# Gate vectors written as rows, an entry with two tiles' first products, and conditioning vectors spread over the heads

## Chip, cores and metric

One program on one core of a Trainium2 chip. The metric is device time in microseconds (us) of one execution; three runs of the kernel before gave a median of 1038.4 us (1037.4 to 1039.1).

## The reference

One layer on a sequence of 512 tokens of width 1024, in float32: a half-weight SwiGLU feed-forward (FFN1), a token mixing with four mLSTM heads and four HGRN2 heads, and a second half-weight feed-forward (FFN2). Each sub-layer normalises its input, scales and shifts it with vectors computed from a conditioning vector `c`, and adds its normalised output through a gate that comes from `c` too:

```python
sc = jax.nn.silu(c)
mod = (sc @ ada_w[l] + ada_b[l])[:, None, :]
(sh1, sc1, g1, sh2, sc2, g2, sh3, sc3, g3) = jnp.split(mod, N_MOD, axis=-1)

y = rmsnorm(h, ffn1_pre_g[l]) * (1.0 + sc1) + sh1
y = swiglu(y, ffn1_w_gate[l], ffn1_w_up[l], ffn1_w_down[l])
h = h + FFN_RESIDUAL_WEIGHT * g1 * rmsnorm(y, ffn1_post_g[l])
# the same with sh2, sc2, g2 around token_mix (no half weight), and with sh3, sc3, g3 around the second swiglu
```

## The kernel before

Every weight matrix is multiplied in a split form: a tile is loaded raw (512 KB for 128 partitions x 1024), ScalarE (ACT) writes its rounded part `h_...`, VectorE (DVE) the remainder `l_...`, and TensorE (PE) makes three matmuls for each product, high by high (L111), low by high (L112), high by low (L113). Raw tiles, conditioning blocks included, go round four buffers, split pairs round four more; loads are issued by SyncE (SP) in program order, each when its buffer is free. Each engine runs its queue in order; a scheduler put the instructions into that order by their place in the program and by what they depend on, and an instruction that waits holds everything behind it on its engine.

**FFN tiles (`seven`, L262 to L401).** The first three of 22 feature tiles of a feed-forward are plain products. From tile 3 on, a tile is made with seven half-size products (`p1` to `p7`), all of 128x256 outputs, 12 matmuls each, in two accumulators `pA` and `pB`. The names end in the tile: `pAa3` is `pA` of FFN1's tile 3, `pAb3` of FFN2's. A tile's raw halves are `Ra` and `Rb`. `prep1` splits `Ra` (`h1`, `l1`) and rounds half of `Rb` (`h4`); `prep2` forms differences of `Ra` and `Rb` in place (L312 to L315), `prep3` and `prep4` split these (`h3`, `l3` and `h2`, `l2`), `prep5` makes `l4` with an accumulating load. `open` takes the accumulators. `p1` and `p2` need only `h1`, `l1` and the activations; `p6`, `p5`, `p7` need sums of activations too (`Shi`, `Slo`, `S[2]`) and `h2`, `h3`; `p4` and `p3` close the tile. In the loop the next tile `v` is prepared and its `p1` and `p2` run between `p7` and `p4` of the current tile `w`. `w.p7` leaves through an ACT copy (L352, `s3`), `w.p6` through another (L344, `s12`).

**Conditioning vectors (`ada`, L126).** One of 72 blocks of `ada_w` (512 KB) is loaded, DVE reduces it in four pieces against `sc` (L137) and adds the pieces (L141): 128 entries of one vector. FFN1's loop does one block for each tile, its load (L123) issued one tile ahead.

**Gates.** When the eight blocks of a gate are there, `gate_rows(s)` (L161) scales the 128x8 tile on DVE (L164, L165) and writes it to memory (`gd0` to `gd2`) through ACT's DMA queue (L167). `gate_load` (L171) loads it back over all 128 partitions as `G0` to `G2`, first used by the down projection's exit (L478, `ysba`, `ysbm`, `ysbb`). For FFN1 the program has `gate_rows(0)` after the tiles; the scheduler lets its pieces run as soon as the last block of FFN1's gate is reduced, still between the tiles.

**Mixing.** 24 projections `ft0` to `ft23` of 512 features each run PE while two chains of small steps (one for an HGRN2 head, one for an mLSTM head) are let in between. `evac_conv` turns the projections of a head's queries and keys into `qk` (DVE, L891 to L894), whose product is L931. `gates_b` and `gates_c` make the recurrences' row vectors. The mixing gate's eight blocks `ada(1, 2, j)` are let in by `spend` (L1009), load and reduction together: five in a head, so all eight and `gate_rows(1)` lie in the first two heads.

Of the kernel before, what the change touches and what calls it, by code (L numbers as in the profile page):

```python
# [7 lines left out]
F32 = mybir.dt.float32  # L8
# [6 lines left out]
P = 128  # L15
# [3 lines left out]
KT = D // P  # L19
# [14 lines left out]
def layer_kernel(ctx: ExitStack, tc: tile.TileContext, x, c, cols, gate_b,  # L34
                 ident_d, masks_d, causal_d, ada_w, wgu1, wd1, w_ft, w_vh, w_mv, w_out, wgu2, wd2, out):
    nc = tc.nc

    const = ctx.enter_context(tc.tile_pool(name="const", bufs=1))
    small = ctx.enter_context(tc.tile_pool(name="small", bufs=3))
# [19 lines left out]
    def tr_tile(name):  # L59
        return psum.tile([P, 512], F32, tag="tr", name=name, bufs=2)  # L60
# [13 lines left out]
    ident = const.tile([P, P], F32, name="ident")  # L74
# [84 lines left out]
    gates = {}  # L159

    def gate_rows(s):  # L161

        g = modc[s][:, 2, :]
        nc.vector.tensor_tensor(out=g, in0=g, in1=col[:, 152 + s * KT:152 + (s + 1) * KT], op=ALU.mult)  # L164
        nc.vector.tensor_scalar(g, g, (1.0 if s == 1 else 0.5) * float(D) ** 0.5, None, ALU.mult)  # L165
        gates[s] = dram.tile([1, D], F32, name=f"gd{s}")
        nc.scalar.dma_start(gates[s].rearrange("o (j p) -> p (o j)", p=P), g)  # L167

    def gate_load(s):
        row, gates[s] = gates[s], small.tile([P, D], F32, tag="G", name=f"G{s}", bufs=1)  # L170
# [91 lines left out]
    def seven(hp, tag, f0, wgu, y, S, hT, sum4, ahead, extra):  # L262
# [104 lines left out]
        w, v = W[:2]  # L367
        w.load()
        v.load()
        w.prep1()  # L370
        w.open()
        w.p1()
        w.p2()
        for fn in (S[2], w.prep2, w.prep3, w.prep4, sum4, w.prep5):
            fn()
        for f in range(f0, NF - 1):
            w, v = W.pop(0), W[0]
            w.p6()
            if f + ahead < NF:
                W.append(Tile(f + ahead))  # L380
            if f + 2 < NF:
                W[1].load()
            v.prep1()
            w.p5()
            v.prep2()
            w.p7()
            v.prep3()
            v.open()
            v.p1()
            v.p2()  # L390
            v.prep4()
            w.p4()
            v.prep5()
            w.p3()
            if extra:
                extra.pop(0)()
        w = W[0]
# [105 lines left out]
    def ffn1():  # L503
        with tc.tile_pool(name="hT1", bufs=1) as hp:
# [93 lines left out]
            for n_ in range(3, 3 * 7, 3):  # L598
                extra.insert(n_ - 1, lambda: None)
            todo = seven(hp, "a", START_F, wgu1, y, (*S, sums), hT, sum4, 2, extra)  # L600
            while extra:
                extra.pop(0)()

            def pump():
                if todo:
                    todo.pop(0)()

            gate_rows(0)
            rest = staged(mods[3:])
            rest.insert(14, lambda: ada_scale(1))  # L610
# [6 lines left out]
    def mix(y, later, mods):  # L617
        with ExitStack() as mc:
# [50 lines left out]
            def proj_feat(ft, evac):  # L669
                u = k3(unit(w_ft[ft], 1024, f"ft{ft}"))  # L670
                ps = mm_tile(f"pft{ft}")
                for k in range(KT):
                    mm3(ps, (u[0][:, k, :], u[1][:, k, :]), yk(k), k == 0, k == KT - 1)
                    if k in (3,):
                        pump()
                evac(ps)
                pump()
# [310 lines left out]
            def h_qf(hd):  # L988
                proj_feat(hd, H[hd][0])
                proj_feat(4 + hd, H[hd][1])  # L990
                H[hd][3]()

            def h_g(hd):
                proj_feat(16 + hd, H[hd][2])
                H[hd][4]()

            def m_qk(hd):
                M[hd][5]()
                proj_feat(8 + hd, M[hd][0])
                proj_feat(12 + hd, M[hd][1])  # L1000
                M[hd][3]()

            def m_g(hd):
                proj_feat(20 + hd, M[hd][2])
                M[hd][4]()

            rest = [lambda j=j: ada(1, 2, j) for j in range(KT)] + [lambda: gate_rows(1), lambda: None, lambda: gate_load(1)]
            rest = mods + rest
            def spend(n):  # L1009
                for _ in range(n):  # L1010
                    if len(rest) > 1:
                        rest.pop(0)()

            h_qf(0)
            for hd in range(NH):
                m_qk(hd)
                spend(2)
                h_g(hd)
                spend(1)
                m_g(hd)  # L1020
                spend(2)
                if hd + 1 < NH:
                    h_qf(hd + 1)
            last = rest.pop()
# [11 lines left out]
    def ffn2(y, later):  # L1036
        with tc.tile_pool(name="hT2", bufs=1) as hp:
# [56 lines left out]


            todo = seven(hp, "b", FF2_F, wgu2, y, (Shi, Slo, lambda: None), hT, sum4, 3, [])

            def pump():
                if todo:
                    todo.pop(0)()  # L1100

            rest = [lambda j=j: ada(2, 2, j) for j in range(KT)] + [lambda: gate_rows(2), lambda: gate_load(2)]
            rest = rest[:1] + [lambda: None] + rest[1:]
            down(wd2, None, "b", 2, None, rest=rest, split=splitter(hp, "b", hT), pump=pump)

    ffn2(*mix(*ffn1()))


# [73 lines left out]
```

## Time and profile before

| | |
|---|---|
| median of three runs | 1038.4 us |
| the profiled execution | 1042.26 us |
| its span from first to last instruction | 1040.5 us |
| its mean granted TensorE clock | 0.991 of full speed |
| PE busy | 999.7 us, 96% of the span |
| DVE busy | 776.6 us, 75% |
| ACT busy | 500.7 us, 48% |
| longest waits of PE | 7.2 us, 5.3 us (the start), 3.2 us, 3.0 us, 1.8 us, 1.6 us |

All times are from the profiled execution, from the start of its span. FFN1's entry into the seven-product tiles is at 56 to 81 us, its tiles run to about 261 us, its down projection follows; mixing's projections lie between about 440 and 640 us, FFN2's entry between 720 and 800 us, its down projection from about 900 us. A wait belongs to the engine that stood still and names what released it. An engine's idle time costs something only where the chain that sets the end passes through it; here PE's idle time does, as PE is busy 96% of the span.

### The profile page before, as it was taken

Reading aid. Unit: us, or ns where it says so; the run is one execution under the profiler, and the core shown is the slowest. Engines: PE = TensorE matmul, PEld = TensorE weight load, DVE = VectorE, ACT = ScalarE, POOL = GpSimd, SP = SyncE. Lnnn points to the kernel's source line nnn. Section 1 sums busy time; section 2 is a strip of 40 time slices with the busy share of each in tenths; the row PEclk is TensorE's granted clock in tenths of the full one; section 3 lists DMA queues with packets and bytes.
Section 4 is the critical chain, followed back from the end, with each engine's and each line's share of the span. In section 5 each row is a group of like instructions: output and inputs, shape, how many; then the busy total and the mean of one; then the engine's idle time right before and its main releaser. Section 6 shows DMA issues by size and latency. Waiting matters only on the chain.

```text
span 1040.5 us, 16627 instructions
## 1 busy us (share of the span) xinstructions
PE 999.7 (96%) x6356; PEld 895.7 (86%) x6356; DVE 776.6 (75%) x1700; ACT 500.7 (48%) x876; POOL 105.7 (10%) x142
## 2 busy tenths in 40 slices
PE   6989999799999999998999999999999999999997
PEld 4779999799878887977888887889999999988886
DVE  6998987688967877289777676599777878992423
ACT  5566555466513255334524232366566766651421
POOL 1001101010000021012232222020000110000000
PEclk9999999899999999999999999999999999999999
DMA  9846655565556823255322121252445545554312
GB/s 334 294 125 174 182 153 118 163 161 167 194 192 225 285 94 117 90 197 163 101 62 81 62 79 44 61 143 81 120 127 139 127 138 134 163 182 140 101 42 81
DMA packets 48429, 146.60 MB, mean 141 GB/s; under 512 B 8278, under 2 KB 8662, under 8 KB 48348
## 3 DMA queue, kind: packets, MB, share of 16 engines
q1 hardware_dynamic: 39468, 135.40, 40.3%
q0 software_dynamic: 5472, 9.96, 6.5%
q8 instruction: 50, 0.82, 0.3%
q10 hardware_dynamic: 3408, 0.17, 0.2%
q14 instruction: 31, 0.25, 0.1%
HBM read 143.39 MB, written 2.12 MB: 140 GB/s over the span
## 4 chain that ended last, share of the span: by engine, by line
PE 67%; DVE 18%; DMA 8%; issue 3%; ACT 2%; POOL 1%; SPq 0%; DVEq 0%; POOLq 0%; ACTq 0%
DMA a<-in_ada_w_dram 7%; PE pdb L112 4%; PE pdb L111 4%; PE pdb L113 4%; PE pAb L111 4%; PE pft L113 3%; PE pAb L113 3%; DVE a L137 3%; PE pft L111 3%; PE pft L112 3%; PE pAb L112 3%; DVE l_a L301 3%; PE pda L112 3%; PE pda L113 3%; PE pda L111 3%
## 5 line engine op out<-in xcount | busy, mean ns | idle before, releaser
L137 DVE CUSTOM_DVE_ANT_0 a<-a,sc 128x256 f32<-128x256 f32 x216 | 81.8, 422 | 0.0
L111 PE MATMUL pft<-yhi,h_ft 128*128 128x512 f32 x192 | 79.5, 414 | 0.0
L113 PE MATMUL pft<-yhi,l_ft 128*128 128x512 f32 x192 | 76.4, 398 | 0.0
L112 PE MATMUL pft<-ylo,h_ft 128*128 128x512 f32 x192 | 75.7, 394 | 0.0
L107 DVE TENSOR_TENSOR l_db<-r_db,h_db 128x1024 fp32r<-128x1024 f32 x22 | 26.8, 1223 | 33.2 <-ACT h_db L106 33.1
L111 PE MATMUL pAa<-yhi,h_a 128*128 128x256 f32 x152 | 43.4, 286 | 7.7 <-ACT s3a L352 7.7
L111 PE MATMUL pAa<-Shi,h_a 128*128 128x256 f32 x152 | 43.3, 285 | 4.7 <-ACT h_a L300 3.0
L300 ACT CAST h_a<-Raa 128x512 fp32r<-128x512 f32 x76 | 44.3, 618 | 6.9 <-DVE Raa L315 5.9
L301 DVE TENSOR_TENSOR l_b<-Rab,h_b 128x1024 fp32r<-128x1024 f32 x38 | 46.1, 1219 | 0.1
L300 ACT CAST h_b<-Rab 128x512 fp32r<-128x512 f32 x76 | 43.7, 618 | 3.4 <-PE pub L112 1.6
L301 DVE TENSOR_TENSOR l_a<-Raa,h_a 128x1024 fp32r<-128x1024 f32 x38 | 45.2, 1219 | 0.0
L106 ACT CAST h_da<-r_da 128x1024 fp32r<-128x1024 f32 x22 | 23.1, 1049 | 43.9 <-DMA r_da<-in_wd_dram 24.9
L106 ACT CAST h_db<-r_db 128x1024 fp32r<-128x1024 f32 x22 | 23.1, 1048 | 43.4 <-PE pdb L113 40.0
L113 PE MATMUL pAa<-yhi,l_a 128*128 128x256 f32 x152 | 43.2, 284 | 0.6 <-DVE l_a L301 0.6
L107 DVE TENSOR_TENSOR l_ft<-r_ft,h_ft 128x1024 fp32r<-128x1024 f32 x24 | 29.1, 1220 | 19.5 <-ACT h_ft L106 18.4
L113 PEld LDWEIGHTS pft<-yhi,l_ft 128*128 128x128 f32 x192 | 36.4, 190 | 8.3 <-DVE l_ft L107 0.2
L106 ACT CAST h_ft<-r_ft 128x1024 fp32r<-128x1024 f32 x24 | 24.9, 1045 | 38.6 <-PE pft L112 30.1
L111 PE MATMUL pBa<-yhi,h_a 128*128 128x256 f32 x152 | 43.2, 284 | 0.0
L113 PE MATMUL pAa<-Shi,l_a 128*128 128x256 f32 x152 | 42.8, 281 | 0.4 <-DVE l_a L301 0.4
L113 PE MATMUL pBa<-yhi,l_a 128*128 128x256 f32 x152 | 43.0, 283 | 0.0
L112 PE MATMUL pBa<-ylo,h_a 128*128 128x256 f32 x152 | 43.0, 283 | 0.0
L112 PE MATMUL pAa<-ylo,h_a 128*128 128x256 f32 x152 | 43.0, 283 | 0.0
(408 smaller groups left out, 3625.1 us busy)
## 6 DMA issues: line engine op xcount, KB each, us to landing
a<-in_ada_w_dram SPq DMA_DIRECT2D x70, 512.0 KB, 4.4
r_ft<-in_w_ft_dram SPq DMA_DIRECT2D x24, 512.0 KB, 3.7
r_da<-in_wd_dram SPq DMA_DIRECT2D x22, 512.0 KB, 4.5
r_db<-in_wd_dram SPq DMA_DIRECT2D x22, 512.0 KB, 4.6
RbRb<-in_wgu_dram SPq DMA_DIRECT2D x20, 512.0 KB, 3.7
Raa<-in_wgu_dram SPq DMA_DIRECT2D x19, 512.0 KB, 4.4
Rab<-in_wgu_dram SPq DMA_DIRECT2D x19, 512.0 KB, 3.6
RbG<-in_wgu_dram SPq DMA_DIRECT2D x18, 512.0 KB, 3.5
```

What stands on the lines that cost most here:

```text
L106: nc.scalar.copy(hi, raw)
L107: nc.vector.tensor_tensor(out=lo, in0=raw, in1=hi.bitcast(F32), op=ALU.subtract)
L111: nc.tensor.matmul(ps, lhs[0], rhs[0], start=start, stop=False, **kw)
L112: nc.tensor.matmul(ps, lhs[0], rhs[1], start=False, stop=False, **kw)
L113: nc.tensor.matmul(ps, lhs[1], rhs[0], start=False, stop=stop, **kw)
L137: nc.vector.tensor_tensor_reduce(out=raw[:, sl], in0=raw[:, sl], in1=sc[:, sl], scale=1.0, scalar=init if q == 0 else 0.0, op0=ALU.mult, o ...
L300: nc.scalar.copy(hl[0][:, sl], raw[:, sl])
L301: tt(out=hl[1], in0=raw, in1=hl[0].bitcast(F32), op=ALU.subtract)
```

## The change

`gate_rows` turns the 128x8 gate on PE into 8x128 (`ptg`, by a transpose into one of the two `tr` accumulators), copies it to a new 8-row tile `gt` on DVE, and writes it by SP as eight pieces of 512 bytes; the write on ACT's queue goes. In `seven`, `prep1`, `open`, `p1` and `p2` of the first two tiles are recorded one after the other before the rest, and the loop's first round skips them for its second tile. In `mix`, the spends around a head are 1 and 1 instead of 2, 1 and 2, so that two blocks fall to each of the four heads; `gate_rows(1)` then comes after the last projection and `gate_load(1)` with the output projection.

```diff
         gates[s] = dram.tile([1, D], F32, name=f"gd{s}")
-        nc.scalar.dma_start(gates[s].rearrange("o (j p) -> p (o j)", p=P), g)
+        pt = tr_tile(f"ptg{s}")
+        nc.tensor.transpose(pt[:KT, :P], g, ident)
+        gt = small.tile([P, P], F32, tag="gt", name=f"gt{s}", bufs=1)[:KT, :]
+        nc.vector.tensor_copy(gt, pt[:KT, :P])
+        nc.sync.dma_start(gates[s].rearrange("o (j p) -> (o j) p", p=P), gt)
...
-        w.prep1()
-        w.open()
-        w.p1()
-        w.p2()
+        for t in (w, v):
+            t.prep1()
+            t.open()
+            t.p1()
+            t.p2()
...
-            v.prep1()
+            if f > f0:
+                v.prep1()
             w.p5()
             v.prep2()
             w.p7()
             v.prep3()
-            v.open()
-            v.p1()
-            v.p2()
+            if f > f0:
+                v.open()
+                v.p1()
+                v.p2()
...
-                spend(2)
+                spend(1)
                 h_g(hd)
+                m_g(hd)
                 spend(1)
-                m_g(hd)
-                spend(2)
```

**SP's queue at FFN1's gate.** Names: `a_1_0_3` is the load of a block of set 1, kind 0, number 3; `r_da_0_1` a raw tile of FFN1's down projection. Before:

```order
L123 DMA a_1_0_3_3053<-in_ada_w_dram 128x1024
L171 DMA G0_3241<-gd0_3037 128x1024
L100 DMA r_da_0_1_3107<-in_wd1_dram 128x1024
L123 DMA a_1_0_4_3117<-in_ada_w_dram 128x1024
L100 DMA r_da_0_2_3149<-in_wd1_dram 128x1024
L123 DMA a_1_0_5_3159<-in_ada_w_dram 128x1024
L100 DMA r_da_0_3_3191<-in_wd1_dram 128x1024
L123 DMA a_1_0_6_3201<-in_ada_w_dram 128x1024
L100 DMA r_da_0_4_3233<-in_wd1_dram 128x1024
L100 DMA r_da_0_5_3267<-in_wd1_dram 128x1024
```

After:

```order
L123 DMA a_1_0_3_3057<-in_ada_w_dram 128x1024
L100 DMA r_da_0_1_3111<-in_wd1_dram 128x1024
L123 DMA a_1_0_4_3121<-in_ada_w_dram 128x1024
L100 DMA r_da_0_2_3153<-in_wd1_dram 128x1024
L123 DMA a_1_0_5_3163<-in_ada_w_dram 128x1024
L100 DMA r_da_0_3_3195<-in_wd1_dram 128x1024
L123 DMA a_1_0_6_3205<-in_ada_w_dram 128x1024
L100 DMA r_da_0_4_3237<-in_wd1_dram 128x1024
L171 DMA gd0_3037<-gt0_3040 8x128
L100 DMA r_da_0_5_3271<-in_wd1_dram 128x1024
L123 DMA a_1_0_7_3279<-in_ada_w_dram 128x1024
L175 DMA G0_3245<-gd0_3037 128x1024
```

`G0` moves from before the down projection's second tile to between its sixth and seventh, with `gd0` three places ahead of it. On PE, the transpose `ptg0` stands just before the first matmul of that projection.

**DVE at FFN1's entry.** Names: `l1_a3` and `l1_a4` are remainders of tiles 3 and 4, `hT1` and `Slo` the sums of activations, `Raa3` the in-place differences of tile 3. Before:

```order
L301 TENSOR_TENSOR l1_a3_578<-Raa3_569,h1_a3_577 128x1024
L252 TENSOR_TENSOR hT1_122<-sga_1_563,ps_s3_286 128x512
L252 TENSOR_TENSOR hT1_122<-sga_2_566,ps_s5_300 128x512
L590 TENSOR_TENSOR Slo_559<-hT1_122,Shi_558 128x1024
L587 TENSOR_TENSOR hT1_122<-hT1_122 128x1024
L340 TENSOR_TENSOR ga3_588<-pBa3_586,s12a3_587 128x256
L587 TENSOR_TENSOR hT1_122<-hT1_122 128x1024
L590 TENSOR_TENSOR Slo_559<-hT1_122,Shi_558 128x1024
L314 TENSOR_TENSOR Raa3_569<-RbRb3_573,Raa3_569 128x512
L301 TENSOR_TENSOR l2_a3_635<-RbRb3_573,h2_a3_634 128x1024
L315 TENSOR_TENSOR Raa3_569<-Raa3_569 128x512
L594 TENSOR_TENSOR ylo0_125<-hT1_122,yhi0_124 128x4x256
```

After:

```order
L594 TENSOR_TENSOR hT1_122<-hT1_122 128x1024
L256 TENSOR_TENSOR hT1_122<-sga_1_563,ps_s3_286 128x512
L256 TENSOR_TENSOR hT1_122<-sga_2_566,ps_s5_300 128x512
L305 TENSOR_TENSOR l1_a3_578<-Raa3_569,h1_a3_577 128x1024
L305 TENSOR_TENSOR l1_a4_616<-Raa4_571,h1_a4_615 128x1024
L597 TENSOR_TENSOR Slo_559<-hT1_122,Shi_558 128x1024 x2
L344 TENSOR_TENSOR ga3_588<-pBa3_586,s12a3_587 128x256
L594 TENSOR_TENSOR hT1_122<-hT1_122 128x1024
L318 TENSOR_TENSOR Raa3_569<-RbRb3_573,Raa3_569 128x512
L344 TENSOR_TENSOR ga4_626<-pBa4_624,s12a4_625 128x256
L319 TENSOR_TENSOR Raa3_569<-Raa3_569 128x512
L305 TENSOR_TENSOR l2_a3_673<-RbRb3_573,h2_a3_672 128x1024
```

`l1_a3` stands behind one sum (L594) and two `hT1` products (L256) more, `l1_a4` comes up from four places behind `l2_a3` to right after `l1_a3`, and `l2_a3` has `l1_a4`, a `ga4` and the second `Raa3` ahead of it that came later before. On PE the 24 matmuls of tile 4's `p1` and `p2`, four of which stood before tile 3's `p5` and `p6` and twenty behind them, all stand before these. At FFN2's entry the 24 of tile 4 move from behind tile 3's `p7` to before its `p6`, and nothing else moves on PE there.

**DVE in mixing, where the first head's keys are made.** `cv4` is the convolution of the keys, `qk4` its result, `a_1_2_5` a block of the mixing gate. Before:

```order
L891 SCALAR_TENSOR_TENSOR cv4_4800<-pft12_4766,col_90,cv4_4800 128x511
L809 COPY_PREDICATED A0_4689<-masks_4155,pl0_3_4852 128x512
L137 ISA a_1_2_5_5259,part1_2_5_5261<-a_1_2_5_5259,sc_83,col_90 128x256
L137 ISA part1_2_5_5261 128x1
L137 ISA a_1_2_5_5259,part1_2_5_5261<-a_1_2_5_5259,sc_83 128x256
L137 ISA part1_2_5_5261 128x1
L137 ISA a_1_2_5_5259,part1_2_5_5261<-a_1_2_5_5259,sc_83 128x256
L137 ISA part1_2_5_5261 128x1
L137 ISA a_1_2_5_5259,part1_2_5_5261<-a_1_2_5_5259,sc_83 128x256
L137 ISA part1_2_5_5261 128x1
L820 TENSOR_TENSOR qq0_4686<-qq0_4686,tb0_4691 128x16x16
L894 SCALAR_TENSOR_TENSOR qk4_4801<-qk4_4801,cv4_4800 128x512
```

After:

```order
L898 SCALAR_TENSOR_TENSOR cv4_4804<-pft12_4770,col_90,cv4_4804 128x509
L107 TENSOR_TENSOR l_ft5_5066<-r_ft5_5063,h_ft5_5065 128x1024
L898 SCALAR_TENSOR_TENSOR cv4_4804<-pft12_4770,col_90,cv4_4804 128x510
L137 ISA a_1_2_2_5239,part1_2_2_5241<-a_1_2_2_5239,sc_83,col_90 128x256
L137 ISA part1_2_2_5241 128x1
L898 SCALAR_TENSOR_TENSOR cv4_4804<-pft12_4770,col_90,cv4_4804 128x511
L827 TENSOR_TENSOR qq0_4690<-qq0_4690,tb0_4695 128x32x8
L816 COPY_PREDICATED A0_4693<-masks_4159,pl0_3_4848 128x512
L901 SCALAR_TENSOR_TENSOR qk4_4805<-qk4_4805,cv4_4804 128x512
L137 ISA a_1_2_2_5239,part1_2_2_5241<-a_1_2_2_5239,sc_83 128x256
```

The four pieces of `a_1_2_5` that stood before `qk4` are gone from there; the first piece of `a_1_2_2` stands before the convolution's last step, its other three behind `qk4`.

## Rows read from the trace of the kernel before

**Rows 1.** The page's first part: busy time of an engine, share of the span, instructions
```profile
PE 999.7 (96%) x6356; PEld 895.7 (86%) x6356; DVE 776.6 (75%) x1700; ACT 500.7 (48%) x876; POOL 105.7 (10%) x142
```

**Rows 2.** Waits of PE (line, releaser: total us, times, longest)
```profile
PE pAa L111 <- ACT s3a L352: 7.7, 2, 7.2
...
PE pqk L931 <- DVE qk L894: 3.2, 1, 3.2
PE pAa L111 <- ACT h_a L300: 3.0, 1, 3.0
...
PE pvm L742 <- DVE rowb L735: 1.8, 1, 1.8
PE pAa L111 <- ACT s12a L344: 1.6, 1, 1.6
```

**Rows 3.** Chain of waits, 160 to 200 us (start, us, what)
```profile
156.69 5.07 DMA a<-in_ada_w_dram
...
176.33 12.85 DMA a<-in_ada_w_dram
```

**Rows 4.** DMA in 165 to 200 us: 40 slices; queues; issues with median landing
```profile
GB/s 103 370 201 192 337 112 356 140 0 0 0 12 33 21 9 26 9 19 19 87 194 386 407 288 220 68 19 0 0 0 0 0 84 229 281 5 98 360 323 375
...
q10 hardware_dynamic: 1040, 0.00, 1.7%
...
a<-in_ada_w_dram SPq DMA_DIRECT2D x2, 512.0 KB, 8.5
```

**Rows 5.** Line 167's transfers and their landing, us min/median/max
```profile
L167 ACTq DMA_DIRECT2D gd<-modc x3: 367/378/389, 168.6 to 939.1; - x3
...
DMA to landing us min/median/max: 5.4/6.4/11.7
```

**Rows 6.** ACT, 160 to 196 us (start, us, line, operation, [idle before])
```profile
169.12 0.62 ACT L306 CAST h_a<-RbG 128x512 fp32r<-128x512 f32 x1 [1.43 <-DVE ga L362]
```

**Rows 7.** PE, 189 to 200 us
```profile
192.32 0.58 PE L111 MATMUL pAa<-yhi,h_a 128*128 128x256 f32 x1 [7.21 <-ACT s3a L352]
...
198.20 0.28 PE L111 MATMUL pAa<-Shi,h_a 128*128 128x256 f32 x1
```

**Rows 8.** Windows (busy us of each engine, granted clock, DMA share, GB/s)
```profile
56.00:81.00 25.00, 20.57 (x149) 19.12 (x148) 24.64 (x40) 16.79 (x33) 0.87 (x1) 0.93 0.44 116
192.00:198.00 6.00, 5.68 (x26) 5.68 (x27) 4.93 (x12) 2.73 (x7) 0.00 (x0) 0.50 0.47 139
199.00:205.00 6.00, 6.00 (x53) 6.00 (x52) 5.93 (x11) 4.24 (x9) 0.87 (x1) 1.00 0.52 137
720.00:800.00 80.00, 80.00 (x682) 80.00 (x681) 62.25 (x87) 51.14 (x103) 6.07 (x7) 1.00 0.48 126
```

**Rows 9.** Users of the gate tile G, and its loads' landing
```profile
L478 DVE TENSOR_TENSOR ysba<-pda,G x4: 681/688/692, 310.7 to 328.4; 128x512 f32<-128x512 f32 x4
...
L478 DVE TENSOR_TENSOR ysbm<-pdm,G x4: 684/692/692, 658.8 to 662.7; 128x512 f32<-128x512 f32 x4
...
L478 DVE TENSOR_TENSOR ysbb<-pdb,G x4: 686/692/692, 957.6 to 975.4; 128x512 f32<-128x512 f32 x4
...
DMA to landing us min/median/max: 5.4/5.9/6.4
```

**Rows 10.** PE, 54 to 72 us
```profile
64.87 0.48 PE L111 MATMUL pAa<-Shi,h_a 128*128 128x256 f32 x1 [3.01 <-ACT h_a L300]
```

**Rows 11.** DVE, 54 to 72 us
```profile
64.08 1.22 DVE L301 TENSOR_TENSOR l_a<-RbRb,h_a 128x1024 fp32r<-128x1024 f32 x1
```

**Rows 12.** Chain of waits, 430 to 512 us
```profile
470.75 6.20 DMA a<-in_ada_w_dram
```

**Rows 13.** DVE, 430 to 510 us
```profile
476.98 0.82 DVE L137 CUSTOM_DVE_ANT_0 a<-a,sc,col 128x256 f32<-128x256 f32 x1 [0.71 <-DMA a<-in_ada_w_dram]
```

**Rows 14.** PE, 476 to 482 us
```profile
479.93 1.13 PE L931 MATMUL pqk<-qk,qk 128*128 128x128 f32 x8 [3.19 <-DVE qk L894]
480.89 0.49 PE L768 MATMUL pktkm<-ident,qk 128*128 128x128 f32 x3
```

## The prediction

> **What bounds the kernel now.** I read the page's busy times first, then PE's waits, then the chain of waits, PE, DVE and ACT rows and the windows around each place that the change touches. PE is busy 999.7 us, 96% of the span [rows 1]: time can come from PE's idle time, from stretches at the lower clock, or not at all. Five of its waits lie where the change works: 7.2, 3.2, 3.0, 1.8 and 1.6 us [rows 2]. The wait at the start of the program it does not touch.
>
> **Gate rows.** The reader is to see the largest wait as the end of a chain that starts at the gate. ACT issues the write of the 128x8 gate at 168.6 us; of the three such writes the slowest lands after 11.7 us [rows 5]. In 165 to 200 us its queue has 1,040 packets for 4 KB, a packet for each of the 1,024 numbers, and for eight slices of 0.9 us, from about 175 to 182 us, all queues together move 9 to 33 GB/s, where 200 to 400 are usual [rows 4]. The conditioning block issued at 176.33 lands 12.85 us later; the one of the tile before, at 156.69, took 5.07 [rows 3]. DVE stands at its reduction, the differences queue behind it, ACT's casts behind these, and PE stands 7.21 us until 192.32 [rows 7]. Then the granted clock is 0.50, that is 1.2 GHz [rows 8]: 27 matmuls start from 192.32 to 198.20, 5.88 us [rows 7], where the next stretch starts 53 in 6.0 us, 0.113 each [rows 8], so they should take 3.1; I count 2.7 lost, with a little off for small gaps. Next, ACT's queue held: the write waits for the scaled gate, the cast behind it starts after 1.43 us idle [rows 6], and PE's wait of 1.6 us for an ACT copy [rows 2] follows at 170.7. Of that I take 0.7 (0 to 1.6, as another wait may come last).
>
> The write is now eight pieces of 512 bytes, from SP, at the start of the down projection, with nothing of the tiles around it. The gate's two DVE steps stay; ACT loses its issue. So 7.2 + 2.7 + 0.7 = 10.6 us go. What is late next in that tile is the block's load by its usual duration: a neighbour's 5.07 us hid, as PE does not wait in the other tiles. If it hides only in part, 8 remains; if the copy's wait goes whole, 11.5.
>
> New there: a transpose of a 128x8 tile on PE. The nearest row is three transposes of 128x128 in 0.49 us [rows 14], 0.16 each: 0.5 for three gates at most, nothing if they fall beside a wait; I take 0.25 on PE's own path. The three DVE copies hide under DVE's idle quarter [rows 1]. On SP, `gd0` waits for the copy (about 263 us) and `G0` for `gd0` to land; three loads and those behind them wait with it. The nearest price of such a landing is the gate loads' 5.4 to 6.4 us [rows 9]; as a bound from below I use nothing, since the old write's 5.4 [rows 5] is for 128 times as many pieces. `G0` then lands by 276 at the latest and is first used at 310.7; for `G1` I get about 645 against 658.8, since `gd1` stands behind the last output tiles' loads. `G2` stands behind the fourth load of the second half; I estimate that it lands at about 960, 2.4 us after its first use at 957.6 [rows 9]. That use is a DVE step at the exit of the first half, with PE in the next half's other accumulators for many us, so I cost it at 0; without that cover it would be those 2.4, up to 5.
>
> **FFN1's entry.** In 56 to 81 us PE is busy 20.57 of 25, DVE 24.64 [rows 8]: this is a DVE-bound stretch, and reordering PE gains only what DVE lets it. PE waits 3.01 us at 64.87 for `h3` of tile 3 [rows 10]. The change puts twenty matmuls of tile 4 (24 in all, 24 x 0.118 = 2.8 us) into that hole. In return `l2_a3`, which starts at 64.08 [rows 11], gets `l1_a4` (1.22), a `ga4` (about 0.4) and a `Raa3` (about 0.7) ahead of it: some 2.0 to 2.3 us later, and tile 3's `p5` can't end before. 2.8 less 2.0 is 0.8; the wait at 64.87 also cost clock, the window's mean is 0.93 [rows 8], or at most 25 x 0.07 = 1.8 us, of which I give back 0.2. I take a gain of 1.0. Bounds: a gain of 3.0, the whole wait, if DVE is no limit, and a loss of 1.5 if `l1_a3`, now 2.3 us later, stops PE early and the clock falls for the 24 matmuls that follow.
>
> **FFN2's entry.** PE is busy 80.00 of 80 us [rows 8], there is nothing to gain. The 24 matmuls that lay between tile 3's `p7` and `p4` covered the ACT copy between them; only four are left, 0.5 us, against a copy and its turn-around of about 0.7. Cost 0.2 (0 to 0.7).
>
> **Mixing.** The wait of 3.2 us is at 479.93: PE waits for `qk4` [rows 14], which stands on DVE behind the four pieces of `a_1_2_5`. Its load is issued at 470.75 and takes 6.20 us [rows 12]; DVE stands 0.71 for it at 476.98 [rows 13], then needs four pieces. Those pieces go; one piece of another block, whose load goes out about 3 us earlier, stands there instead and may wait up to 0.9. I leave 0.7 of the 3.19: 2.5 gained. The wait of 1.8 for `rowb` [rows 2] stays but for 0.3, as a weight remainder (1.2) takes the place of the reductions ahead of it. Against these, four blocks are now reduced in heads three and four, where DVE has room; I take 0.5 for loads that come late. Sum 2.3. Bounds: 5.5, when all of 3.2 and 1.8 and some clock go; -3, when one new wait like that of 479.93 comes.
>
> **A rule on queues.** The 1,024 small writes and the late load ran together, and by the rows I make the one the other's cause. The Trainium skill, "DMA: Bandwidth & Descriptors", says in its section "Queues, rings and completion order" that an engine takes its queues in turn, a packet at a time; by that rule small packets leave another queue its turns, the block's load would not have been held by them, and the sum would be 10 us smaller (the first rival). Its section "Specifications" says that below 512 bytes the engine reads, modifies and writes, by which they are dear packets and the sum stands. The trace, with 12.85 beside 5.07 us, fits the second.
>
> **Sum.** 10.6 + 1.0 + 2.3 - 0.2 - 0.25 = 13.4 us off the profiled execution, 1042.3 to 1028.9. The median of three runs lies 3.9 us below that execution, so 1038.4 less 13.4: 1025.0 us.
>
> **Rivals.** First, the load at 176.33 was late for another reason. For it: the write's packets make only 1.7% of the engines' time there [rows 4], and the tiles' accumulating loads (L326) run beside it. Against it: those run in every tile, the block before took 5.07 us [rows 3], and the slow stretch ends within 2 us of the write's landing (168.6 + 11.7). PE would keep its 7.2 and 2.7: 1038.4 - 13.4 + 9.9 = 1034.9.
>
> Second, FFN1's entry turns into a loss at the lower clock: its 144 matmuls at twice the time for a fifth of them, and a 2.3-us stop, 3.4 + 2.3 = 5.7, with the mixing gaining nothing: 1025.0 + 1.0 + 5.7 + 2.3 = 1034.0. For it speaks DVE's 24.64 of 25; against it, that the same DVE work is done in all.
>
> Third, slower: the blocks now spread over heads two to four are loaded and reduced without being loaded ahead, and DVE stands for each, in front of the step for which PE waits, as at 479.93. The price of one is 3.19 us and, where PE falls to the lower clock, the 2.7 us of 192.32: 5.9. All six later blocks: 35 us would be the end; three are 17.7, and give 1025.0 + 2.3 + 17.7 = 1045. It decides from three full waits up. Against it: DVE waited only 0.71 itself there, and heads three and four have no other blocks.
>
> Fourth, no change: the first rival together with a loss of 2 to 4 us at the entry or in mixing: 1037 to 1039.
>
> **Chances and range.** Forecast 0.72 (its own range 1020 to 1031), first rival 0.12, second 0.05, third 0.05, fourth 0.06. A difference of under 0.2%, 2.1 us, can't be told from no change here. Faster: 0.72 + 0.12 + 0.05 = 0.89; same 0.06; slower 0.05. The range of 8 in 10 reaches from 1019.5 (gains of 11.5, 3.0 and 5.0 less 0.5) to 1035.5, with the first two rivals in it.
>
> **What would show it.** Right: no wait of PE and a clock of 1.00 at 185 to 205 us, and that block's load near 5 us; the eight-piece write lands within some 6 us; no 3.0-us wait at 65 but shorter ones before `l1_a3` and `l2_a3`; under 1 us before the first `pqk`; `ysbb` a little later with no PE wait. Wrong: a wait of many us still at that tile; a window at 56 to 81 us with a mean clock below 0.9; PE waits of over 2 us at a `qk` of a later head.

## The result

Four runs of the changed kernel took 1026.6 us in the median (1022.5 to 1027.2) against 1037.9 of the kernel before, a ratio of 0.988 (95%: 0.985 to 0.991): 11.3 us by the medians, 12.4 by the ratio. 1025.0 was forecast. Two later series of it, on other chips, gave 0.986 (0.984 to 0.989) and 0.982 (0.979 to 0.986).

The profiled execution took 1022.45 us, 19.8 less than the one of before; the medians differ by only 11.3. So this pair of traces shows more than an average pair would, and part of what follows is to find out why. Along the program the pair parts like this (a name's last matmul, before and after, from the PE rows):

| | before | after | difference | so this stretch |
|---|---|---|---|---|
| `pAa4`, FFN1's entry | 85.10 | 82.96 | -2.1 | -2.1 |
| `pAa10` | 145.12 | 142.32 | -2.8 | -0.7 |
| `pAa15`, past the gate | 206.49 | 191.79 | -14.7 | -11.9 |
| `pda_1_3`, FFN1's end | 388.83 | 373.88 | -15.0 | -0.3 |
| `po0`, mixing's first head | 502.73 | 482.70 | -20.0 | -5.1 |
| `pub_2_1`, FFN2's plain tiles | 724.38 | 704.21 | -20.2 | -0.1 |
| `pBb21`, FFN2's tiles | 915.35 | 895.45 | -19.9 | +0.3 |

### The profile page after: what moved, and what is told of

Read it like the earlier page. It is cut to its first block, busy times and chain, and to the rows that moved or that the text cites. A ratio compares the mean times of both kernels' runs of the same rounds, so it can differ in the third digit from the quotient of the medians.

```text
span 1020.7 us, 16635 instructions
## 1 busy us (share of the span) xinstructions
PE 994.5 (97%) x6359; PEld 890.4 (87%) x6359; DVE 777.7 (76%) x1703; ACT 496.9 (49%) x874; POOL 102.8 (10%) x142
## 4 chain that ended last, share of the span: by engine, by line
PE 83%; DVE 10%; ACT 2%; issue 1%; DMA 1%; POOL 1%; SPq 0%; DVEq 0%; POOLq 0%; ACTq 0%
PE pdb L111 4%; PE pdb L112 4%; PE pdb L113 4%; PE pda L112 4%; PE pda L111 4%; PE pda L113 4%; PE pAb L111 4%; PE pAa L111 4%; PE pAb L113 4%; PE pAb L112 3%; PE pAa L113 3%; PE pft L111 3%; PE pft L113 3%; PE pft L112 3%; PE pAa L112 3%; PE pBb L111 3%
## 5 line engine op out<-in xcount | busy, mean ns | idle before, releaser
L111 PE MATMUL pAb<-yhi,h_b 128*128 128x256 f32 x152 | 42.8, 281 | 0.0
L111 PE MATMUL pAb<-Shi,h_b 128*128 128x256 f32 x152 | 42.5, 280 | 0.0
L111 PE MATMUL pBb<-yhi,h_b 128*128 128x256 f32 x152 | 42.5, 280 | 0.0
L113 PE MATMUL pBb<-yhi,l_b 128*128 128x256 f32 x152 | 42.4, 279 | 0.0
```

The lines of the kernel that those rows point to most:

```text
L111: nc.tensor.matmul(ps, lhs[0], rhs[0], start=start, stop=False, **kw)
L113: nc.tensor.matmul(ps, lhs[1], rhs[0], start=False, stop=stop, **kw)
```

## The profile after

PE's busy time, and its waits after the program's start:

```profile
PE 994.5 (97%) x6359; PEld 890.4 (87%) x6359; DVE 777.7 (76%) x1703; ACT 496.9 (49%) x874; POOL 102.8 (10%) x142
```

```profile
PE pAa L111 <- ACT h_a L304: 1.7, 2, 1.3
...
PE pl L815 <- DVE rm L980: 1.3, 1, 1.3
PE pvm L749 <- DVE rowb L742: 1.2, 1, 1.2
...
PE pAa L113 <- DVE l_a L305: 0.8, 1, 0.8
...
PE pAa L111 <- ACT s12a L348: 0.5, 1, 0.5
```

Against [rows 2], the waits for `s3a` and `qk` are gone, that for `h_a` went from 3.0 to 1.7, that for `s12a` from 1.6 to 0.5. The windows show the same, and the clock:

```profile
56.00:81.00 25.00, 21.44 (x167) 19.86 (x166) 24.74 (x37) 17.70 (x35) 0.87 (x1) 1.00 0.48 117
160.00:185.00 25.00, 25.00 (x214) 25.00 (x214) 23.09 (x48) 14.41 (x32) 1.77 (x2) 1.00 0.60 165
185.00:205.00 20.00, 20.00 (x172) 20.00 (x171) 17.53 (x32) 12.31 (x28) 1.75 (x2) 1.00 0.68 183
434.60:440.00 5.40, 4.16 (x23) 2.94 (x22) 5.40 (x14) 2.83 (x3) 0.00 (x0) 1.00 0.04 15
440.00:445.00 5.00, 5.00 (x32) 4.41 (x31) 2.40 (x9) 1.19 (x3) 0.00 (x0) 1.00 0.86 268
720.00:800.00 80.00, 80.00 (x682) 80.00 (x681) 63.93 (x91) 52.52 (x107) 7.06 (x9) 1.00 0.52 133
```

From 160 to 205 us PE is busy without a break at full clock, where before it stood 7.21 us and ran the next 27 matmuls at 1.2 GHz [rows 7, 8]. The block that DVE waited for is there in time; DVE waits 0.72 and 1.61 us for two blocks and PE does not notice:

```profile
176.00 0.49 DVE L137 CUSTOM_DVE_ANT_0 a<-a,sc,bs 128x256 f32<-128x256 f32 x1 [0.72 <-DMA a<-in_ada_w_dram]
...
188.39 0.49 DVE L137 CUSTOM_DVE_ANT_0 a<-a,sc,bs 128x256 f32<-128x256 f32 x1 [1.61 <-DMA a<-in_ada_w_dram]
```

## The experiments

Ratios are to runs of the kernel before on the same chip, with 95% intervals. On these chips it took 1040.7 to 1041.7 us in the median, some 3 us more than in the first series, so that the gains of an expectation are to be compared with the ratios, not its times with the medians.

**The gate rows alone** (the other two edits undone).

```diff
-        nc.scalar.dma_start(gates[s].rearrange("o (j p) -> p (o j)", p=P), g)
+        nc.tensor.transpose(pt[:KT, :P], g, ident)
+        nc.vector.tensor_copy(gt, pt[:KT, :P])
+        nc.sync.dma_start(gates[s].rearrange("o (j p) -> (o j) p", p=P), gt)
```

> Only the gate rows are changed (transpose, eight pieces, from SP); entry and mixing as before. Theory A, the 4-byte write delayed a block's load and by it PE: no wait near 190 us, PE 10 to 12 us earlier from there on, in all 1026 to 1029 us. Rival B, the load was late for another reason: PE still waits some 7 us in that tile, 1037 to 1039 us. Rival C, the gain of the whole change comes from entry and mixing: 1034 us or more.

Ratio 0.992 (0.990 to 0.994), 1031.2 us: 8.4 us by the ratio, 10.5 by the medians. Of PE's waits after the start these two are the longest; in the gate's tile and the next none is over 0.6 us:

```profile
PE pAa L111 <- ACT h_a L304: 3.0, 1, 3.0
PE pqk L935 <- DVE qk L898: 2.8, 1, 2.8
```

Theory A holds in its mechanism: from `pAa10` to `pAa15` this trace takes 49.4 us where the one of before takes 61.4. In size 8.4 is less than the 10 to 12 of that theory.

**The entry alone, twice.**

```diff
-        w.prep1()
-        w.open()
-        w.p1()
-        w.p2()
+        for t in (w, v):
+            t.prep1()
+            t.open()
+            t.p1()
+            t.p2()
```

> Only the entry of the seven-product tiles is changed, in both feed-forwards. Theory A: FFN1's entry ends 2 us earlier, the late block's wait near 190 us stays, FFN2's entry gains nothing: 1036 to 1037 us. Rival B: what is gained at the entry is taken back at the late block, which waits for its load and not for PE: 1038 us, no change.

> The entry change alone once more, for a second trace. In its first trace every matmul of FFN2's tiles started 0.113 us after the one before, in all other traces 0.118, which is 0.37 us a tile and 6.4 us in all. Theory A, this pace belongs to an execution and not to the kernel: this trace shows 9.89 us a tile in FFN2 and its median is 1 to 3 us below the kernel before. Rival B, it belongs to this program (its order with its layout): 9.52 us a tile again, and a median 5 to 8 us below.

Ratios 0.994 (0.992 to 0.996) and 0.996 (0.994 to 0.998), 6.2 and 4.3 us: more than the 1 to 2 that theory A gave the entry, and rival B's no change is out. The first trace's FFN1 entry ends 1.8 us earlier (`pAa4` at 83.34), the second's 0.6 (84.49); the wait in the gate's tile stays in both. The first ran FFN2's tiles at 9.52 us each, the second at 9.89: the same program, so the pace is an execution's. The second series is nearer to what the entry is worth, with luck still in it: 2.1 us of its trace's gain lie in mixing, which this edit does not touch.

**The spread alone.**

```diff
-                spend(2)
+                spend(1)
                 h_g(hd)
+                m_g(hd)
                 spend(1)
-                m_g(hd)
-                spend(2)
```

> Only the mixing's blocks are spread, two to a head; the gate rows are written as before (4-byte pieces, from ACT's queue). Theory A: the waits of 1.8 and 3.2 us in mixing shrink or go, 3 to 5 us in the trace from 437 to 500 us, in all 1033 to 1036 us. Rival B: the second gate's 4-byte write, now late in mixing, delays the output projection's loads and takes 2 to 5 us back: 1037 to 1039 us.

Ratio 0.997 (0.995 to 0.999), 3.3 us (1.5 to 5.1), theory A: from FFN1's end to `po0` its trace takes 109.2 us against 113.9, and what B was to take back is not seen in the time. PE waits for no `qk` any more; at the gate, where the 4-byte write stays, it does:

```profile
PE pAa L111 <- ACT s3a L352: 3.7, 2, 3.3
...
PE pAa L111 <- ACT s12a L344: 2.3, 3, 1.8
```

**FFN2's entry alone** (the entry edit for FFN2 only).

```diff
+        both = tag == "b"
+        for t in (w, v) if both else (w,):
...
+            if f > f0 or not both:
```

> The kernel before with the new order at FFN2's entry alone. Theory A, this order costs 0.2 to 0.5 us by a short wait behind tile 3's p7 and does nothing else: median within 1 us of the kernel before, runs no wider than its own (1037.4 to 1045.7 so far). Theory B, the short wait draws the pace of FFN2's tiles anew, so that a part of the executions run them at 9.52 us a tile: runs in two groups some 6 us apart, the lower one at 1031 to 1035 us, median 1 to 5 us below the kernel before.

Ratio 1.001 (0.999 to 1.002): theory A; B's two groups did not show in twelve runs. `pub_2_1` to `pBb21` is 191.24 us against 190.97 before.

Its chain of waits and PE rows also show the gate's tile once more, with the 4-byte write and nothing else changed ahead of it:

```profile
177.38 9.89 DMA a<-in_ada_w_dram
```

```profile
190.41 0.58 PE L111 MATMUL pAa<-yhi,h_a 128*128 128x256 f32 x1 [2.71 <-ACT s3a L352]
```

With the 4-byte write the block's load and PE's wait go together in five traces, and both vary a good deal:

| trace with the 4-byte write among the tiles | load, us | PE's wait, us |
|---|---|---|
| before | 12.85 | 7.21 |
| entry alone, first | 12.37 | 7.25 |
| entry alone, second | 11.22 | 5.58 |
| spread alone | 10.43 | 3.25 |
| FFN2's entry alone | 9.89 | 2.71 |

**The 4-byte write at the new place.**

```diff
-        nc.tensor.transpose(pt[:KT, :P], g, ident)
+        nc.tensor.matmul(pt[:, :KT], ident, g, start=True, stop=True)
...
-        nc.sync.dma_start(gates[s].rearrange("o (j p) -> (o j) p", p=P), gt)
+        nc.sync.dma_start(gates[s].rearrange("o (j p) -> p (o j)", p=P), gt)
```

> The changed kernel, but the gates are written again as 1,024 numbers of 4 bytes each (128x8, through a product with the identity and a DVE copy), at the places and from the queue of the eight-piece write. Theory A, the shape of the write is what holds other loads: the loads of the down projection beside gd0 land late (10 us and more instead of about 4.5), G0 later; whether PE waits depends on the slack there: 1026 to 1034 us. Rival B, it was the place among the tiles and on ACT's queue: these loads land as in the changed kernel, time as the changed kernel.

Ratio 0.988 (0.985 to 0.991), 1030.3 us. The down projection's raw tile that was issued 0.9 us ahead of `gd0` lands after 10.0 us; the same tile of the changed kernel (second line) takes 4.4. For the two loads right behind `gd0` the trace has no landing.

```profile
r_da<-in_wd_dram SPq DMA_DIRECT2D x1, 512.0 KB, 10.0
```

```profile
r_da<-in_wd_dram SPq DMA_DIRECT2D x1, 512.0 KB, 4.4
```

The first `gd` is issued at 249.9, `G0`, which waits for it, at 261.8 (landings of both kinds together in the last row):

```profile
L171 SPq DMA_DIRECT2D gd<-gt x3: 377/378/387, 249.9 to 933.4; - x3
L175 SPq DMA_DIRECT2D G<-gd x3: 326/327/327, 261.8 to 946.3; - x3
...
DMA to landing us min/median/max: 3.9/11.4/13.0
```

Of the traffic in 245 to 270 us (40 slices), eleven slices in a row, 254.4 to 261.2 us, move 20 to 118 GB/s, from 4.5 us after the write's issue to its end:

```profile
GB/s 361 387 374 413 184 20 72 111 393 321 262 270 311 296 139 85 33 26 52 20 39 92 98 118 66 66 138 105 98 210 243 229 223 354 419 420 406 295 275 295
```

and PE has a wait there that the changed kernel has not:

```profile
296.44 0.50 PE L112 MATMUL pda<-l_da,hsaX3h 128*128 128x512 f32 x1 [1.06 <-DVE l_da L107]
```

So theory A: the shape makes other transfers slow at this place and on SP's queue too. That the wait of 1.06 us comes from it is not shown: it stands 35 us behind the write, and one trace with eight-piece writes (`gt` in the ring, below) has 0.43 us at the same place. In time the kernel is not told apart from the changed one.

**Eight pieces among the tiles.** Of the changed kernel, the first gate is turned and written from ACT's queue among the tiles (at 197.6 us, about three tiles of 10 us behind where the 4-byte write was).

```diff
+            step8 = extra[8]
+            extra[8] = lambda: (step8(), gate_rows(0))
...
-            gate_rows(0)
```

> The changed kernel, but the first gate is turned and written as eight pieces from ACT's queue as soon as its last block is reduced, among FFN1's tiles, one or two tiles after where the 4-byte write was. Theory A, shape: loads of the blocks and tiles beside it land in 4 to 6 us, PE waits under 1 us there, time within 2 us of the changed kernel. Rival B, place: blocks land late again, PE waits 5 us or more, 1033 to 1038 us.

Ratio 0.985 (0.983 to 0.987), 1025.5 us. The loads issued in 190 to 225 us land in their usual time (issues: KB each, median us to landing), and PE's one wait of any length in 185 to 215 us is short. The block issued 7 us behind the write, at 204.64, has no landing in the trace, but DVE reduces it from 208.05, so it took 3.4 us at most:

```profile
Raa<-in_wgu_dram SPq DMA_DIRECT2D x3, 512.0 KB, 3.7
RbG<-in_wgu_dram SPq DMA_DIRECT2D x2, 512.0 KB, 3.5
RbRb<-in_wgu_dram SPq DMA_DIRECT2D x2, 512.0 KB, 4.2
```

```profile
208.05 0.48 DVE L137 CUSTOM_DVE_ANT_0 a<-a,sc,bs 128x256 f32<-128x256 f32 x1 [0.26 <-DMA a<-in_ada_w_dram]
```

```profile
198.59 0.39 PE L111 MATMUL pAa<-Shi,h_a 128*128 128x256 f32 x1 [0.71 <-ACT s12a L348]
```

Theory A. Shape was the cause; the place decided what it cost. The shape changed in two ways at once, 8 pieces for 1,024 and 512 bytes for 4; which of the two counts these runs do not separate.

**The changed kernel twice more, and two variants.** One variant puts `gt` into an existing ring, the other leaves FFN2's entry as it was.

```diff
-        gt = small.tile([P, P], F32, tag="gt", name=f"gt{s}", bufs=1)[:KT, :]
+        gt = small.tile([P, T], F32, tag="x2", name=f"gt{s}")[:KT, :P]
```

> The changed kernel once more, for a second trace. Its first profiled execution took 1022.5 us, three others 1026.2 to 1027.2. Theory A, some executions have one more wait of about 4 us at one place: this trace, if it is one of the slower ones, shows one stretch of about 4 us that the other has not. Rival B, the difference is spread over many matmuls: no single place, each stage longer by a few tenths of a per cent.

> The changed kernel, beside the next two on one chip. In the traces so far a 128x256 matmul follows the one before after 0.118 or 0.113 us, and the pace changes only at a wait of PE. Theory A, the pace is drawn anew at such a wait in each execution: this kernel's runs spread over 1020 to 1030 us, the fast ones being those with the quick pace in a feed-forward. Rival B, the pace belongs to the program: FFN2's tiles at 9.89 us as in both traces of this kernel, and all runs within 1025 to 1030 us.

> The changed kernel with the turned gate in a buffer of an existing ring, so that no buffer lies elsewhere than in the kernel before. Order on PE is the same. If the pace of 0.113 us belongs to order and layout together (rival B of the entry run): FFN2's tiles at 9.52 us, 6 us below the changed kernel, 1019 to 1021 us. If it belongs to an execution (theory A): as the changed kernel, 1025 to 1028 us, with one or the other pace in its trace.

> The changed kernel with the turned gate in an existing ring, once more and beside the changed kernel. Theory A, the pace is drawn in each execution: median within 3 us of the changed kernel, FFN2's tiles at 9.89 or 9.52 us. Rival B, order and layout together set it: FFN2's tiles at 9.52 us again and a median 4 to 7 us below the changed kernel.

> The changed kernel, but FFN2's entry in the order of the kernel before (tile 4's first products after tile 3's p7); FFN1's entry as changed. My prediction had the new order in FFN2 cost 0.2 us. Theory A: the 0.2 to 0.5 us come back at FFN2's entry and nothing else changes but the pace drawn: median within 3 us of the changed kernel. Rival B, the short wait in FFN2's entry is what sets the pace of all its tiles: without it they go at one pace in every run, and the median lies 4 us or more off the changed kernel's, with a smaller spread.

The changed kernel: 1026.9 us (1023.4 to 1029.9) and 1022.8 (1017.6 to 1028.9). `gt` in the ring: 1020.2 (1016.4 to 1026.9) and, beside the second of these, 1027.2 (1024.6 to 1028.8). Without FFN2's new order: 1026.4 (1024.4 to 1027.9). None beats the changed kernel beyond these spreads. The first series of `gt` in the ring looked like 6 us gained; the second, beside the changed kernel, did not bear it out. FFN2's tiles took 9.52 us each in the third trace of the changed kernel and 9.89 in its first two, 9.52 and 9.89 in the two of `gt` in the ring: the pace is drawn in each execution. Without FFN2's new order `pub_2_1` to `pBb21` is 190.98 us, so the 0.3 come back and nothing else. The slower trace of the changed kernel (1028.1 us) differs from its first by 1.3 us at FFN1's entry, 1.7 over the rest of FFN1 and 3.1 in mixing: neither one place, as I had expected, nor evenly spread. At the first and the last of these it is for the most part the clock: the mean granted clock is 0.93 in 56 to 81 us and 0.50 in 442 to 448 us, where the first trace has 1.00 at both; between them there are a few short waits more.

## Why the prediction was right, by its steps

- **Gate rows, 10.6 us.** The chain was right: the pair gives 11.9 us between tiles 10 and 15, the waits of 7.2 and 1.6 gone, the clock full. The size was some 2 us too large, since the trace of before held the longest of the five loads above; my 7.2 and 2.7 were one draw. Alone the edit is worth 8.4 by the ratio, and from `pAa10` to FFN1's end the five traces with the 4-byte write among the tiles take 242.0 us in the mean, the nine without it 233.1. [rows 5] I read too far, for its view takes the writes and the loads of `G` together: the landing of 11.7 us is that of `gd2` (issued at 939.1, `G2` at 950.8), the 5.4 that of a `G`, and the trace gives none for `gd0`. The slow slices carry the argument without it, and the 11.9 us in the run with the late 4-byte write bear it out.
- **First rival (the load late for another reason), 0.12.** Excluded: five traces with that write among the tiles, loads of 9.9 to 12.9 us; in the nine traces without it the two blocks at that place took 3.4 to 5.7. The rule of queues that take turns ("DMA: Bandwidth & Descriptors", "Queues, rings and completion order" in the Trainium skill), as I read it, would have kept SP's load going beside ACT's write; in this kernel the load did not keep going, though the two were on different queues all five times. What holds the load inside the DMA engines no run here shows.
- **Second rival (the entry a loss at the lower clock), 0.05.** The clock did fall there in six of ten traces with the new order (see FFN1's entry below), but even these end `pAa4` earlier than any with the old one. **Fourth rival (no change), 0.06:** the ratio of 0.988 lies clear of 1.
- **New operations on the path.** `G0` is issued 2.8 us after `gd0`, so the write took at most that:

```profile
L171 SPq DMA_DIRECT2D gd<-gt x3: 291/293/296, 248.7 to 931.9; - x3
L175 SPq DMA_DIRECT2D G<-gd x3: 326/339/425, 251.5 to 934.2; - x3
```

  I had allowed up to 6.4. A transpose held PE up by about 0.11 us, 0.3 for the three gates, where I had 0.25: from the last matmul ahead of `ptg2` to the second behind it are 0.57 us, where two steps of 0.23 are usual. `G2` came late, as forecast, but by more than the 2.4 us that I had: DVE waited 5.0 us for it, PE not at all:

```profile
938.83 0.69 DVE L485 TENSOR_TENSOR ysbb<-pdb,G 128x512 f32<-128x512 f32 x1 [5.01 <-DMA G<-gd]
```

- **FFN1's entry, 1.0 us.** Right in direction, mis-sized: 2.1 in this pair. PE's waits there are now

```profile
59.09 0.39 PE L113 MATMUL pAa<-yhi,l_a 128*128 128x256 f32 x1 [0.81 <-DVE l_a L305]
...
65.56 0.39 PE L111 MATMUL pAa<-Shi,h_a 128*128 128x256 f32 x1 [1.26 <-ACT h_a L304]
...
66.63 0.39 PE L113 MATMUL pBa<-Shi,l_a 128*128 128x256 f32 x1 [0.57 <-DVE l_a L305]
```

  of which the first is for `l1_a3` and the third for `l2_a3`, as named. `l2_a3` starts here:

```profile
65.35 1.22 DVE L305 TENSOR_TENSOR l_a<-RbRb,h_a 128x1024 fp32r<-128x1024 f32 x1
```

  It is 1.3 us later than before [rows 11], not 2.0 to 2.3: a sum of `hT1` moved up on DVE into half a microsecond that was idle. PE's waits there fell from 4.4 to 3.5 us in sum; most of the rest is the clock, whose mean in the window is 1.00 instead of 0.93. I had given back 0.2 of 1.8 for that. But the clock is a draw. The third trace of the changed kernel has the same wait of 1.26 us, and the clock of before:

```profile
65.79 0.39 PE L111 MATMUL pAa<-Shi,h_a 128*128 128x256 f32 x1 [1.26 <-ACT h_a L304]
```

```profile
56.00:81.00 25.00, 21.54 (x155) 19.85 (x154) 23.65 (x33) 16.80 (x34) 1.28 (x2) 0.93 0.46 113
```

  Of the ten traces with the new order, four have 1.00 in this window and end `pAa4` at 82.8 to 83.3; six have 0.93 and end it at 84.1 to 84.6. The four with the old order have 0.93 or 0.86 and end it at 85.1 to 87.4. Against the one old trace with 0.93, that of before, these six gain 0.6 to 1.0 us, about the 0.8 that I had for the order; the full clock gives 1.3 more, and that is the term that I had too small. Over all these traces the gain is 2.3 us to `pAa4` and 3.2 to `pAa10`.
- **FFN2's entry, -0.2.** Measured: 0.1 to 0.3 in the seven traces with the new order and the pace of before.
- **Mixing, 2.3 us.** Mis-sized: 5.1 in this pair, 3.3 alone by the ratio; over all fourteen traces the stretch from FFN1's end to `po0` takes 113.0 us in the mean without the spread (111.8 to 114.2) and 109.9 with it (107.5 to 112.0). I left 0.7 before `qk4` and nothing is left: that wait is 2.5 to 3.2 us in the five traces without the spread and gone in the nine with it. The wait for `rowb` fell from 1.75 to 1.25 in this pair:

```profile
437.91 0.22 PE L749 MATMUL pvm<-ident,rowb 4*128 4x4 f32 x1 [1.25 <-DVE rowb L742]
...
460.50 1.13 PE L938 MATMUL pqk<-qk,qk 128*128 128x128 f32 x8
```

  PE's clock did not fall after it, either, which before cost seven matmuls about double their time (the first line, 455 to 460 us of before; 1.00 here in the windows above). Both are draws, too. Without the spread the wait for `rowb` is 0 to 1.75 us over the traces; with it, it is 0.6 to 1.4, in four of nine with a wait of 1.2 to 1.3 us for `rowv` besides, and in the second trace of the changed kernel the clock behind the two is that of the second line:

```profile
455.00:460.00 5.00, 5.00 (x22) 4.12 (x22) 3.37 (x9) 0.14 (x1) 0.00 (x0) 0.75 0.70 197
```

```profile
442.00:448.00 6.00, 5.73 (x21) 4.84 (x22) 2.88 (x9) 0.18 (x1) 0.00 (x0) 0.50 0.53 137
```

- **Third rival (blocks in later heads stop DVE and PE).** No wait of PE for a `qk` of heads two to four came, in any of the nine traces with the spread.
- **The sum.** 13.4 forecast; 12.4, 14.3 and 18.4 measured by the ratios of three series. The mechanisms were right; that the sum came so near is in part luck, by errors that cancelled: the gate some 2 too large, the entry 2 and mixing 1 too small. Over the fourteen traces the stretches give, in the mean, 9.0 for the gate, 3.2 for FFN1's entry and 3.1 for mixing, less 0.2 at FFN2's entry: 15.1. The edits alone add to 16 to 18 us by the ratios (8.4, 4.3 or 6.2, 3.3), the faster pace in some runs of the entry included. That they add exactly is not shown, for the spread of the runs is as wide.

## What to carry over

Price a write of a thousand 4-byte pieces not by its 4 KB but by the loads that run beside it; turning it on PE first cost PE about 0.1 us. A stall read from one trace is one draw: the same tile's wait was 2.7 to 7.25 us over five. The clock behind a wait is a draw as well: with one order FFN1's entry kept the full clock in four traces and not in six, so a gain of clock that one pair of traces shows is not yet the edit's.

## What was not expected

PE's pace within the seven-product tiles has two values at the same granted clock of 1.00. The changed kernel, in its first trace and in its third (columns as in the windows above):

```profile
740.00:780.00 40.00, 40.00 (x342) 40.00 (x341) 31.75 (x46) 26.15 (x54) 3.46 (x4) 1.00 0.53 133
```

```profile
740.00:780.00 40.00, 40.00 (x356) 40.00 (x355) 33.11 (x48) 26.74 (x56) 3.85 (x5) 1.00 0.54 142
```

342 against 356 matmuls of 128x256 in 40 us, 0.118 or 0.113 us from start to start; a tile takes 9.89 or 9.52 us, FFN2's tiles together 6.5 less. In the traces that I followed the pace changed where PE had a short wait, and held for 170 us where it had none. Which of the two it takes I could not steer: entry alone and `gt` in the ring each showed both, the changed kernel too, and FFN2's entry alone had no group of quick runs among its twelve. It goes with runs some 6 us apart; what sets it stays open.
